# Groups 2 to 4 of an up projection as seven block products for eight, in an fp32 transformer block on one Trainium2 core

## The chip, the core and the metric

The kernel runs on one core of one Trainium2 chip. A core has TensorE (PE; its weight loads are listed apart as PEld), VectorE (DVE), ScalarE (ACT), GpSimd (POOL) and SyncE (SP), and 16 DMA engines. SP issues most loads; POOL issues the DMAs that add to what is already in device memory. The metric is the device time of one execution in microseconds (us).

## The reference

`hybrid_layer` is one transformer block on 512 tokens of width 1024, in fp32. All the input projections are one product, `proj = xn @ w_in`. A gated delta rule (8 heads) and a chunked retention (4 heads) follow, each with a gate and an output projection; then the mix, and an MLP:

```python
mix = (jax.nn.sigmoid(gate_a) * ya + jax.nn.sigmoid(gate_b) * yb) @ w_out
x = x + rmsnorm(mix, n_mix_post)

hn = rmsnorm(x, n_mlp_pre)
ff = jnp.square(jax.nn.relu(hn @ w_up)) @ w_down      # w_up 1024 x 4096, w_down 4096 x 1024
return x + rmsnorm(ff, n_mlp_post)
```

The change is in `hn @ w_up`.

## The kernel before

**Precision.** Each fp32 operand of a large product is split into a high part (rounded to the PE's fp32r) and a low part (the rest). `mm3` (L79) issues three matmuls: high x high, high x low, low x high. Activations are split once and stay on chip. Weights are split when they arrive: `weights` (L86) takes one of the `raw` buffers, has SP load 512 KB into it, and calls `split_weights` (L102), where ACT casts to `whi` (L109) and DVE subtracts to get `wlo` (L110). There are three slots each of `whi` and `wlo`, and two raw buffers, or four where a second pool is in `raw_pools`. The splits have a raised priority in the scheduler, which writes one fixed order of instructions for each engine; engines then work in that order and wait for each other by semaphores.

**Forms of product.** `feature_major` (L146) keeps weights stationary and streams the tokens: its results have features on the partitions. It runs over blocks of 2 x 128 rows of the weights, and inside over four groups of 128 features, each with its own PSUM bank of the pool `psm` (four banks, tag `mm`). `token_major` (L166) keeps activations stationary and streams the weights. A second PSUM pool, `psx`, has three banks with the tag `dl`.

**Seven products for eight.** The value and gate projections of the four retention heads, `values_and_gates` (L768), already use a scheme of the Strassen-Winograd kind. Tokens are halved (256 each), the 1024 rows of the weights are halved (512 each), and a pair of 512-wide column blocks makes up the two column halves: a 2 x 2 by 2 x 2 block product, done with seven block products instead of eight. It needs four sums of feature blocks (`feature_sums`, L752, kept on chip as high and low parts `s1` to `s4`) and four sums of weight blocks. The weight sums are made in device memory by `BlockSums` (L116): SP copies a block into a DRAM tile (`copy`, L127, in two parts), POOL issues DMAs that add other blocks or earlier sums to it (`adds`, L130, eight a set). The copies wait in a list, `trickle`; from the 14th load on each call of `weights` takes one off and puts it behind its own load on SP. The adds are handed out in order by `add_blocks` (L704), behind a marked DMA on POOL. `block_weights` (L139) loads and splits a summed block like any other.

**Order of the work around the change.** Delta rule (to about 500 us), then the retention heads one by one: `scores`, a gate product or the branch partial of the head before, `outputs` with `values_and_gates`. Then the second gate product, the last branch partial, and the mix. The output projection (`row_tiles`, L990) keeps its eight weight blocks split on chip (in buffers of tags `og`, `ff0`, `ff1` and `facc`), and for each tile of 128 tokens `mix_done` adds the residual, normalizes and transposes into `hn`.

The MLP (L1093 to L1136) goes in four groups of 1024 of the 4096 hidden features. For each group the up projection comes first, `feature_major` over two halves of 512 features with eight weight loads in all (the first half of the first group runs twice over 256 tokens, because its last tokens come late), and `square_relu` (L1083) takes each bank: ACT writes relu to `r`, DVE multiplies, ACT casts to the high part, DVE subtracts the low part. Then the down projection, `token_major` over two halves of 512 columns, is added to `facc`. Groups 1 and 3 keep their hidden features in `og` and `ff0`/`ff1`, groups 2 and 4 in the `actT` buffers. The last down projection is `row_tiles` again, with its weights kept in `og`, `ff0`/`ff1` and the place of `hn`; after each token tile comes the last norm and the store.

Of the kernel before, what the change touches and what calls it, by code (L numbers as in the profile page):

```python
# [60 lines left out]
def hybrid_block_kernel(ctx: ExitStack, tc: tile.TileContext, a: dict, out: bass.AP):  # L61
# [10 lines left out]
    trickle = []  # L72
    act = ctx.enter_context(tc.tile_pool(name="act", bufs=2))
# [12 lines left out]
    def weights(src, k0, nk, c0, ncols, keep=None):  # L86

        n = nk * ncols
        i = next(loads)
        pool, tag = raw_pools[i % len(raw_pools)]  # L90
        raw = pool.tile([P, 1024], F32, tag=tag, name="raw", bufs=2)
        load = nc.sync.dma_start(
            raw[:, :n].rearrange("p (k c) -> p k c", k=nk),
            src[k0 * P : (k0 + nk) * P, c0 : c0 + ncols].rearrange("(k p) c -> p k c", p=P),
        )
        if i >= 13 and trickle:
            sums, part, k = trickle.pop(0)
            with tc.issue_after(load.ins):
                sums.copy(part, k)
        return split_weights(raw, n, nk, keep, 200 if i >= 6 else 0)  # L100
# [38 lines left out]
    def block_weights(block):  # L139
# [4 lines left out]
        return split_weights(raw, 1024, 2)  # L144

# [299 lines left out]
    with tc.tile_pool(name="pa", bufs=1) as pa:  # L445
# [255 lines left out]
        vg_sums = [BlockSums(w_in, OFF_VB + h * 512, OFF_GB + h * 512, f"vg{h}") for h in range(4)]  # L701
        adds = itertools.chain.from_iterable(sums.adds() for sums in vg_sums)

        def add_blocks(mark, n):  # L704

            with tc.issue_after(mark.ins):
                for dst, src in itertools.islice(adds, n):
                    tc.keep_in_program_order(nc.gpsimd.dma_start(dst, src, accum_op=ALU.add))

# [26 lines left out]
    with tc.tile_pool(name="pb", bufs=1) as pb_:  # L736
# [10 lines left out]
        def quarter(kh, th):  # L747
            return [x[:, 4 * kh : 4 * kh + 4, 256 * th : 256 * th + 256] for x in xs]

        quarters = {"11": quarter(0, 0), "12": quarter(1, 0), "22": quarter(1, 1)}  # L750

        def feature_sums():  # L752
            full = [pb_.tile([P, 2, 4, 256], F32, tag=f"vr{i}", name="full") for i in range(2)]
            a11, a12, a21, a22 = full[0][:, 0], full[0][:, 1], full[1][:, 0], full[1][:, 1]
            for a, (kh, th) in ((a21, (0, 1)), (a22, (1, 1)), (a11, (0, 0)), (a12, (1, 0))):
                h, l = quarter(kh, th)
                nc.vector.tensor_tensor(a, h, l, ALU.add)
            nc.vector.tensor_tensor(a22, a21, a22, ALU.subtract)
            nc.vector.tensor_tensor(a21, a11, a21, ALU.subtract)
            nc.vector.tensor_tensor(a11, a22, a11, ALU.subtract)  # L760
            nc.vector.tensor_tensor(a12, a12, a11, ALU.add)
            for i, a in enumerate((a22, a11, a21, a12)):
                s = pb_.tile([P, 2, 4, 256], F32R, tag=f"xs{i}", name="xsum")
                nc.scalar.copy(s[:, 0], a)
                nc.vector.tensor_tensor(s[:, 1], a, s[:, 0], ALU.subtract)
                quarters[f"s{i + 1}"] = [s[:, 0], s[:, 1]]

        def values_and_gates(sums, c1, c2, g, out1, out2):  # L768
# [20 lines left out]
            def bank():  # L789
                return [psm.tile([P, T], F32, tag="mm", name="mm") for _ in range(2)]  # L790

            def plain(kh, c):
                return lambda ks: weights(w_in, 4 * kh + 2 * ks, 2, c, 512)

            def multiply(pss, x, wts, first):
                for ks in range(2):
                    product(pss, x, ks, wts(ks), first)

            def total(i):
                return lambda ks: sums.weights(i, ks)  # L800

            a = bank()
            multiply(a, "11", plain(0, c1), True)
            p1 = [tmp("p1") for _ in range(2)]
            with tc.high_priority(400):
                for t in range(2):
                    nc.scalar.copy(p1[t], a[t])
            multiply(a, "12", plain(1, c1), False)
            for t in range(2):
                out1(t, a[t])  # L810
            c = bank()
            multiply(c, "s1", total(1), True)
            with tc.high_priority(400):
                for t in range(2):
                    nc.scalar.copy(g[:, 2 + t, :], c[t])
            b = bank()
            multiply(b, "s3", total(3), True)
            p7 = [tmp("p7") for _ in range(2)]
            with tc.high_priority(400):
                for t in range(2):  # L820
                    nc.scalar.copy(p7[t], b[t])
            multiply(b, "s2", total(2), False)
            for t in range(2):
                nc.vector.tensor_tensor(p1[t], p1[t], b[t], ALU.add)
                nc.vector.tensor_tensor(p7[t], p1[t], p7[t], ALU.subtract)
                nc.vector.tensor_tensor(g[:, 2 + t, :], g[:, 2 + t, :], p1[t], ALU.subtract)
                out2(2 + t)
            d = [psx.tile([P, T], F32, tag="dl", name="dl", bufs=3) for _ in range(2)]
            multiply(d, "22", total(4), True)
            for t in range(2):  # L830
                nc.vector.tensor_tensor(p1[t], p1[t], d[t], ALU.add)
                out1(2 + t, p1[t])
            multiply(c, "s4", plain(1, c2), False)
            for t in range(2):
                nc.vector.tensor_tensor(g[:, t, :], c[t], p7[t], ALU.subtract)
                out2(t)
# [13 lines left out]
        def scores(h):  # L850
            dec = pb_.tile([P, T], F32, tag="dec", name="dec")
            decay = nc.gpsimd.dma_start(dec, a["c_decay"][h])
            if h in (1, 2):
                add_blocks(decay, 8 if h == 1 else 2)
# [69 lines left out]
        for h in range(4):  # L924
# [20 lines left out]
            if h == 0:  # L945
                raw_pools.append((pb_, "ych"))
            rows = outputs(h, scs)
# [4 lines left out]
        for half in range(2):  # L952
            ya.append(pb_.tile([P, 4, T], F32, tag=f"xs{2 + half}", name="ya"))
            nc.gpsimd.dma_start(ya[half], ya_d[:, half * 4 : half * 4 + 4, :])
# [24 lines left out]
    with tc.tile_pool(name="pm", bufs=1) as pm:  # L979
        def broadcast_row(vec, tag):  # L980
            w = pm.tile([P, D], F32, tag=tag, name=tag)
            nc.gpsimd.dma_start(w, vec.partition_broadcast(P))
# [62 lines left out]
        for t in range(4):  # L1045
            nc.gpsimd.dma_start(x2[:, t, :], x_d[t * P : (t + 1) * P, :])
# [36 lines left out]
        def square_relu(ps, hi, lo):  # L1083
            n = ps.shape[1]
            r = pm.tile([P, T], F32, tag="r", name="r", bufs=2)[:, :n]
            nc.scalar.activation(r, ps, AF.Relu)
            nc.vector.scalar_tensor_tensor(r, ps, 0.0, r, ALU.max, ALU.mult)  # L1087
            nc.scalar.copy(hi, r)
            nc.vector.tensor_tensor(lo, r, hi, ALU.subtract)

        wpost = broadcast_row(a["norm_mlp_post"][0], "post")
        facc = pm.tile([P, 4, D], F32, tag="facc", name="facc")
        for grp in range(4):  # L1093
            if grp % 2:
                whole = [act.tile([P, 8, T], F32R, tag="actT", name="actT") for _ in range(2)]
                ff = [[w[:, 4 * half : 4 * half + 4, :] for w in whole] for half in range(2)]
            else:
                ff = [
                    [act.tile([P, 4, T], F32R, tag="og", name="ff") for _ in range(2)],
# [64 lines left out]
```

## Time and profile before

| | |
|---|---|
| time, median of 3 runs | 1392.08 us (1391.12 to 1394.7) |
| profiled execution: time / span | 1392.33 us / 1390.6 us |
| granted PE clock, mean | 0.994 |
| PE / DVE / ACT / POOL busy | 1368.6 / 870.1 / 614.0 / 86.3 us |
| PE matmul instructions | 6670 |
| moved by DMA | 180.08 MB, mean 130 GB/s |
| up projection of group 2 (1121 to 1164.5 us): PE / DVE / ACT busy | 43.50 / 16.83 / 15.70 us |
| value-and-gate products of one head (679.26 to 717.34 us): PE / DVE / ACT busy | 38.08 / 24.42 / 21.53 us |

The span runs from the first to the last instruction; the time of an execution has a little around it. A row of a group of instructions gives its line in the code, its engine, the operation, what it writes and reads, how often, its busy time in us and the mean duration of one in ns. In a timeline row the first number is the start in us, the second the duration, and in brackets stands how long the engine was idle before and what released it. Matmuls are pipelined: their durations overlap, so their cost is the distance from start to start. A row of waits gives who waited for whom, the total in us, how many times, and the longest. A row of a stretch gives its bounds, its length, each engine's busy time with the count of instructions, the granted PE clock, the busy share of the DMA engines and GB/s.

### The profile page before, as it was taken

Reading aid. Unit: us, or ns where it says so; the run is one execution under the profiler, and the core shown is the slowest. Engines: PE = TensorE matmul, PEld = TensorE weight load, DVE = VectorE, ACT = ScalarE, POOL = GpSimd, SP = SyncE. Lnnn points to the kernel's source line nnn. Section 1 sums busy time; section 2 is a strip of 40 time slices with the busy share of each in tenths; the row PEclk is TensorE's granted clock in tenths of the full one; section 3 lists DMA queues with packets and bytes.
Section 4 is the critical chain, followed back from the end, with each engine's and each line's share of the span. In section 5 each row is a group of like instructions: output and inputs, shape, how many; then the busy total and the mean of one; then the engine's idle time right before and its main releaser. Section 6 shows DMA issues by size and latency. Waiting matters only on the chain.

```text
span 1390.6 us, 17607 instructions
## 1 busy us (share of the span) xinstructions
PE 1368.6 (98%) x6670; PEld 1123.1 (81%) x6670; DVE 870.1 (63%) x1539; ACT 614.0 (44%) x1134; POOL 86.3 (6%) x136
## 2 busy tenths in 40 slices
PE   8999999999999999999999999999999999999997
PEld 6888787778887888887888878878788888888886
DVE  5599889954665567477477486675685333343445
ACT  5777564624544323453553443543364333232331
POOL 1112300221021002000000000000000000000000
PEclk8999999999999999999999999999999999999999
DMA  5243624369367448762552443642724233233321
GB/s 159 72 141 120 190 92 158 117 147 235 107 129 159 121 144 168 193 206 76 157 154 84 151 121 91 200 133 68 236 91 135 93 94 104 92 103 94 106 76 61
DMA packets 88311, 180.08 MB, mean 130 GB/s; under 512 B 6079, under 2 KB 19537, under 8 KB 87714
## 3 DMA queue, kind: packets, MB, share of 16 engines
q1 hardware_dynamic: 77264, 148.39, 34.1%
q0 software_dynamic: 10240, 29.32, 10.8%
q8 instruction: 52, 0.85, 0.2%
q10 hardware_dynamic: 722, 1.25, 0.2%
q14 instruction: 33, 0.27, 0.1%
HBM read 173.17 MB, written 39.32 MB: 153 GB/s over the span
## 4 chain that ended last, share of the span: by engine, by line
PE 87%; DVE 6%; DMA 4%; ACT 2%; issue 1%; SPq 0%; DVEq 0%; ACTq 0%
PE mm L84 21%; PE mm L83 21%; PE mm L82 21%; PE mm L779 9%; PE tr L218 2%; DMA raw<-in_w_in_dram 2%; PE dl L779 2%; DVE wlo L110 1%; PE dl L84 1%; PE dl L82 1%; PE dl L83 1%; PE dl L670 1%; DVE c_y L406 1%; PE dl L642 1%; ACT whi L109 1%
## 5 line engine op out<-in xcount | busy, mean ns | idle before, releaser
L110 DVE TENSOR_TENSOR wlo<-raw,whi 128x1024 fp32r<-128x1024 f32 x232 | 283.5, 1223 | 334.9 <-ACT whi L109 334.0
L109 ACT CAST whi<-raw 128x1024 fp32r<-128x1024 f32 x232 | 244.0, 1053 | 452.4 <-PE mm L83 226.8
L84 PE MATMUL mm<-actT,wlo 128*128 128x512 f32 (+1 forms) x528 | 209.2, 396 | 0.0
L83 PE MATMUL mm<-actT,whi 128*128 128x512 f32 (+1 forms) x528 | 207.9, 394 | 1.1 <-DVE actT L252 1.1
L82 PE MATMUL mm<-actT,whi 128*128 128x512 f32 (+1 forms) x528 | 207.3, 394 | 0.6 <-ACT actT L251 0.6
L82 PEld LDWEIGHTS mm<-actT,whi 128*128 128x128 f32 x528 | 100.3, 190 | 20.6 <-ACT actT L251 1.1
L83 PEld LDWEIGHTS mm<-actT,whi 128*128 128x128 f32 x528 | 100.4, 190 | 20.4 <-DVE actT L252 1.3
L84 PEld LDWEIGHTS mm<-actT,wlo 128*128 128x128 f32 x528 | 100.7, 191 | 18.8
L82 PE MATMUL mm<-hn,whi 128*128 128x512 f32 (+1 forms) x288 | 105.6, 367 | 0.6 <-DVE r L1087 0.5
L83 PE MATMUL mm<-hn,whi 128*128 128x512 f32 (+1 forms) x288 | 105.3, 366 | 0.0
L84 PE MATMUL mm<-hn,wlo 128*128 128x512 f32 (+1 forms) x288 | 105.1, 366 | 0.0
L82 PE MATMUL mm<-og,whi 128*128 128x512 f32 x256 | 99.7, 390 | 0.6 <-DVE zz L369 0.6
L83 PE MATMUL mm<-og,whi 128*128 128x512 f32 x256 | 99.6, 389 | 0.0
L84 PE MATMUL mm<-og,wlo 128*128 128x512 f32 x256 | 99.6, 389 | 0.0
L82 PE MATMUL mm<-whi,actT 128*128 128x512 f32 x216 | 86.2, 399 | 0.0
L83 PE MATMUL mm<-wlo,actT 128*128 128x512 f32 x216 | 86.0, 398 | 0.0
L84 PE MATMUL mm<-whi,actT 128*128 128x512 f32 x216 | 85.6, 397 | 0.0
L779 PE MATMUL mm<-whi,xsum 128*128 128x512 f32 x256 | 80.1, 389 | 0.0
L406 DVE SCALAR_TENSOR_TENSOR c_y<-c_raw,convw,c_y 128x512 f32<-128x512 f32 x96 | 70.6, 752 | 3.4 <-ACT c_y L404 2.8
L82 PEld LDWEIGHTS mm<-hn,whi 128*128 128x128 f32 x288 | 54.3, 188 | 10.1 <-DVE r L1087 0.9
L83 PEld LDWEIGHTS mm<-hn,whi 128*128 128x128 f32 x288 | 54.3, 188 | 8.8
L84 PEld LDWEIGHTS mm<-hn,wlo 128*128 128x128 f32 x288 | 54.2, 189 | 8.8
(319 smaller groups left out, 2459.8 us busy)
## 6 DMA issues: line engine op xcount, KB each, us to landing
raw<-in_w_in_dram SPq DMA_DIRECT2D x105, 512.0 KB, 3.8
raw<-in_w_up_dram SPq DMA_DIRECT2D x36, 512.0 KB, 3.8
sums<-in_w_in_dram SPq DMA_DIRECT2D x32, 512.0 KB, 5.4
raw<-sums SPq DMA_DIRECT2D x32, 512.0 KB, 4.1
raw<-in_w_down_dram SPq DMA_DIRECT2D x32, 512.0 KB, 3.7
raw<-in_w_br_a_dram SPq DMA_DIRECT2D x16, 512.0 KB, 4.0
sums<-in_w_in_dram POOLq DMA_DIRECT2D x16, 512.0 KB, 12.3
sums<-sums POOLq DMA_DIRECT2D x16, 512.0 KB, 7.0
```

The costliest lines, as they stand in the source:

```text
L82: nc.tensor.matmul(ps, lh, rh, start=first, stop=False)
L83: nc.tensor.matmul(ps, lh, rl, start=False, stop=False)
L84: nc.tensor.matmul(ps, ll, rh, start=False, stop=last)
L109: nc.scalar.copy(hi[:, :n], raw[:, :n])
L110: nc.vector.tensor_tensor(lo[:, :n], raw[:, :n], hi[:, :n], ALU.subtract)
L218: nc.tensor.transpose(ps, src, ident)
L406: nc.vector.scalar_tensor_tensor(y, raw[:, j : j + T], tap(j), y, ALU.mult, ALU.add)
L642: nc.tensor.matmul(px[:, hh, :], rt[:, nn[hh], :], vx[:, hh, :], start=True, stop=True)
L670: nc.tensor.matmul(po[:, hh, :], at[:, 4 * hh + c, :], vn[:, hh, :], start=True, stop=True)
L779: m = nc.tensor.matmul(pss[t], lhs[i // 2], rhs[i % 2], start=first and k + i == 0, stop=k + i == 5, skip_group_check=not first,)
```

## The change

The scheme of the value and gate projections is made general and used for groups 2 to 4 of the up projection too.

- `seven` takes the place of the body of `values_and_gates` and serves both. The order of products is now 11, s2, 12, s1, s3, 22, s4 (it was 11, 12, s1, s3, s2, 22, s4). The products 11 and 12, and 22, go to `psx` banks, s2 with s3 and s1 with s4 to `psm` banks. Two pairs of temporaries are kept: `p1`, a copy of product 11 and later a running sum, and `u2` = p1 + product s2.
- For the up projection `up_product` keeps the weights stationary and streams 256 tokens: a PSUM bank holds two feature groups of 256 tokens side by side. `squares_up` takes the output blocks: the first (first token half, first column half) straight from PSUM as before; the other three with an addition or subtraction into `r` first.
- Three more `BlockSums` (`up_sums`, from `w_up`): 24 more copies on SP and 24 more adds on POOL, of 512 KB each. The copies are held back (`later_copies`) until the first retention head's gate products are done, and then follow the loads of scores and branch partials in heads 2 to 4 (loads inside `seven` take none). The adds come in batches: 4 behind the decay load of the fourth head, 10 behind the load of `ya`, 10 behind the residual loads and the row `wmlp`.
- Feature sums of `hn`: `sum_quarters` (8 DVE sums of 128 x 1024, 4 ACT casts, 4 DVE subtractions), put on DVE behind the first half of group 1. The plain sums stand in the place of `facc`, the split ones in `og` and `ff0`/`ff1` until the last group.
- All groups keep their hidden features in the `actT` buffers.

The diff, cut to its core:

```diff
-    def weights(src, k0, nk, c0, ncols, keep=None):
+    def weights(src, k0, nk, c0, ncols, keep=None, paced=True):
...
-        if i >= 13 and trickle:
+        if paced and i >= 13 and len(trickle) > later_copies[0]:
...
+    vg_sums = [BlockSums(w_in, OFF_VB + h * 512, OFF_GB + h * 512, f"vg{h}") for h in range(4)]
+    up_sums = [BlockSums(w_up, grp * 1024, grp * 1024 + 512, f"up{grp}") for grp in range(1, 4)]
+    adds = itertools.chain.from_iterable(sums.adds() for sums in vg_sums + up_sums)
...
+    def sum_quarters(xs, full, sums, quarters):
+        a11, a12, a21, a22 = full
+        for a, (kh, th) in ((a21, (0, 1)), (a22, (1, 1)), (a11, (0, 0)), (a12, (1, 0))):
+            h, l = quarter(xs, kh, th)
+            nc.vector.tensor_tensor(a, h, l, ALU.add)
+        nc.vector.tensor_tensor(a22, a21, a22, ALU.subtract)
+        nc.vector.tensor_tensor(a21, a11, a21, ALU.subtract)
+        nc.vector.tensor_tensor(a11, a22, a11, ALU.subtract)
+        nc.vector.tensor_tensor(a12, a12, a11, ALU.add)
+        for i, (a, s) in enumerate(zip((a22, a11, a21, a12), sums)):
+            nc.scalar.copy(s[:, 0], a)
+            nc.vector.tensor_tensor(s[:, 1], a, s[:, 0], ALU.subtract)
+            quarters[f"s{i + 1}"] = [s[:, 0], s[:, 1]]
+
+    def seven(src, c1, c2, sums, product, temp, out):
...
+        p1, u2 = [temp("p1") for _ in range(2)], [temp("u2") for _ in range(2)]
+        a = bank(psx)
+        plain(a, "11", 0, c1, True)
+        with tc.high_priority(400):
+            for t in range(2):
+                nc.scalar.copy(p1[t], a[t])
+        b = bank(psm)
+        summed(b, "s2", 2, True)
+        with tc.high_priority(400):
+            for t in range(2):
+                nc.vector.tensor_tensor(u2[t], p1[t], b[t], ALU.add)
+        plain(a, "12", 1, c1, False)
+        out(0, 0, a)
+        c = bank(psm)
+        summed(c, "s1", 1, True)
+        summed(b, "s3", 3, False)
+        with tc.high_priority(400):
+            for t in range(2):
+                nc.vector.tensor_tensor(p1[t], p1[t], b[t], ALU.add)
+        out(1, 1, c, p1, ALU.subtract)
+        d = bank(psx)
+        summed(d, "22", 4, True)
+        out(1, 0, d, p1, ALU.add)
+        plain(c, "s4", 1, c2, False)
+        out(0, 1, c, u2, ALU.subtract)
...
+        add_blocks(kept, 10)
...
+        with tc.issue_after(rows_in[1].ins):
+            add_blocks(residual, 10)
+        quarters = {"11": quarter(hn, 0, 0), "12": quarter(hn, 1, 0), "22": quarter(hn, 1, 1)}
...
+        def up_product(pss, x, ks, wts, first):
+            wh, wl = wts
+            xh, xl = quarters[x]
+            for f in range(4):
+                fs, ts = slice(f * P, (f + 1) * P), slice(256 * (f % 2), 256 * (f % 2) + 256)
+                for kk in range(2):
+                    k = 2 * ks + kk
+                    lhs, rhs = (wh[:, kk, fs], wl[:, kk, fs]), (xh[:, k, :], xl[:, k, :])
+                    for i in range(3):
+                        m = nc.tensor.matmul(
+                            pss[f // 2][:, ts], lhs[i // 2], rhs[i % 2],
+                            start=first and k + i + f % 2 == 0, stop=k + i == 5, skip_group_check=True,
+                        )
...
+        def squares_up(th, ch, pss, u=None, op=None):
+            for t in range(2):
+                dst = [w[:, 2 * t : 2 * t + 2, 256 * th : 256 * th + 256] for w in ff[ch]]
+                if u is None:
+                    square_relu(pss[t], *dst)
+                else:
+                    r = pm.tile([P, T], F32, tag="r", name="r", bufs=2)
+                    nc.vector.tensor_tensor(r, pss[t], u[t], op)
+                    square_relu(r, *dst, r)
...
         for grp in range(4):
+            whole = [act.tile([P, 8, T], F32R, tag="actT", name="actT") for _ in range(2)]
+            ff = [[w[:, 4 * half : 4 * half + 4, :] for w in whole] for half in range(2)]
+            if grp:
+                pinned = []
+                seven(
+                    w_up, grp * 1024, grp * 1024 + 512, up_sums[grp - 1], up_product,
+                    lambda name: pm.tile([P, T], F32, tag="u", name=name, bufs=4), squares_up,
+                )
```

145 lines of the change are left out of this document (59 added, 86 removed).

## The prediction

> **What bounds the kernel now.** I read the page's head, its shares of engines and the chain that ended last; then what TensorE (PE) waits for; then the stages around the change. The profiled execution took 1392.33 us, 1.73 us more than its span; the median of the three runs, 1392.08, is 0.25 us below it.
>
> ```profile
> span 1390.6 us, 17607 instructions
> PE 1368.6 (98%) x6670; PEld 1123.1 (81%) x6670; DVE 870.1 (63%) x1539; ACT 614.0 (44%) x1134; POOL 86.3 (6%) x136
> PE 87%; DVE 6%; DMA 4%; ACT 2%; issue 1%; SPq 0%; DVEq 0%; ACTq 0%
> PE tr L218 <- DVE o L916: 1.7, 4, 0.4
> PE mm L83 <- DVE keep L110: 0.8, 1, 0.8
> PE mm L82 <- DVE r L1087: 0.5, 1, 0.5
> PE mm L82 <- ACT keep L109: 0.4, 1, 0.4
> PE tr L218 <- DVE fw L1071: 0.3, 1, 0.3
> ```
>
> The last five rows are all of PE's waits from 560 us to the end: 3.7 us. Everything that the change touches lies there. So PE's own time sets the end, a matmul saved is time saved, and a new wait counts in full. Next is what one matmul costs: first and last row of two undisturbed stretches of PE's timeline, both in the first group of the up projection, where the weights are the stationary side as they will be in the new code.
>
> ```profile
> 1050.01 0.28 PE L83 MATMUL mm<-hn,whi 128*128 128x256 f32 x1
> 1052.89 0.28 PE L83 MATMUL mm<-hn,whi 128*128 128x256 f32 x1
> ...
> 1068.67 0.39 PE L83 MATMUL mm<-hn,whi 128*128 128x512 f32 x1
> 1077.51 0.39 PE L83 MATMUL mm<-hn,whi 128*128 128x512 f32 x1
> ```
>
> 24 starts of the 256-column kind in 2.88 us make 0.120 us each; 39 of the 512-column kind in 8.84 us make 0.2267 us. Half the columns cost 53%, not 50%: solved for a fixed part, 13.3 ns a matmul beside 0.4167 ns a column.
>
> **The change, part by part.** (1) *Matmuls.* A group of the up projection has 2 halves x 8 k x 4 features x 3 = 192 matmuls of 512 columns: 192 x 0.2267 = 43.5 us. Seven block products have 7 x 4 k x 4 features x 3 = 336 of 256 columns: 336 x 0.120 = 40.3 us. An eighth of the arithmetic is 5.4 us, but 144 further instructions take 144 x 13.3 ns = 1.9 us of it back. Gain 3.2 us a group, **9.6 us** in three. The new loop issues high x high, high x low, low x high as the old one does, so I take the row without an allowance.
>
> The Trainium skill, TensorE: Matmul & The Clock Gate, section Back-to-back issue gap, gives 262 cycles for 256 columns and 518 for 512, a fixed part of only 6 cycles. At 2.4 GHz (the page's warm clock) that would make the gain (192 x 518 - 336 x 262)/2400 = 4.8 us a group, 14.3 in all. The rows above give 288 and 544 cycles, so the trace disagrees, and the sum goes by the trace.
>
> (2) *Weight splits, DVE and ACT.* A group now has 8 blocks of 512 KB to split into high and low; it will have 14, one per 24 matmuls (2.88 us of PE).
>
> ```profile
> 1154.10 1.05 ACT L109 CAST whi<-raw 128x1024 fp32r<-128x1024 f32 x1 [4.38 <-PE mm L83]
> 1155.18 1.23 DVE L110 TENSOR_TENSOR wlo<-raw,whi 128x1024 fp32r<-128x1024 f32 x1 [4.21 <-ACT whi L109]
> 1340.37 4.63 DVE L110 TENSOR_TENSOR keep<-raw,keep 128x1024 fp32r<-128x1024 f32 x4 [0.23 <-ACT keep L109]
> 706.01 1.28 DVE L824 TENSOR_TENSOR p<-p,mm 128x512 f32<-128x512 f32 x2
> ...
> 715.79 1.23 DVE L110 TENSOR_TENSOR wlo<-raw,whi 128x1024 fp32r<-128x1024 f32 x1 [0.29 <-ACT whi L109]
> 1142.08 0.62 ACT L1088 CAST actT<-r 128x512 fp32r<-128x512 f32 x1 [0.25 <-DVE r L1087]
> ```
>
> Back to back a split costs DVE 4.63/4 = 1.16 us and an operation on 512 columns 1.28/2 = 0.64. A split starts when PE leaves its slot (first row) and is whole 2.3 us later. With three slots, it is needed two blocks after its start: 5.76 - 2.3 = 3.5 us to spare.
>
> DVE per group: 14 x 1.16, and on 512 columns 2 for u2, 2 for p1, 4 for the first output block and 6 for each of the three others, 26 x 0.64: 32.9 us of 40.3 (82%). ACT: 14 x 1.05 and 12 evictions of 0.62: 22.1 us. Neither becomes the bound on average; what counts is the crowd at the end. From the end of s3 (28.8 us into the group) DVE has p1 (1.3 us), the second output block (3.8) and two splits (2.3): 7.4 us in the 5.76 us of the sixth product. A bank is complete 1.4 us before its product ends, so DVE starts early: about 0.3 us of arrears. Then the third output block and two splits, 6.2 us in 5.76, leave some 0.7 us. At 40.3 us the down projection starts and wants the bank read by the last output after 12 matmuls (2.7 us). That bank is complete at 38.9 and is read about 1 to 2 us later: just in time. In the last group the down product uses two row tiles at once and wants it after 6 matmuls (1.4 us). I take 0.3 us a boundary, **+0.9 us**; bounds: 0, and 3.8 us a boundary (a whole output ahead of the read).
>
> (3) *Feature sums in group 1.* DVE gets 8 sums and 4 low parts of the form of the split, 12 x 1.16 = 13.9 us; ACT 4 x 1.05. They queue behind the last eviction of the first half:
>
> ```profile
> 1059.69 0.41 DVE L1089 TENSOR_TENSOR ff<-r,ff 128x256 fp32r<-128x256 f32 x1
> core 0: us, PE busy (x) PEld busy (x) DVE busy (x) ACT busy (x) POOL busy (x), PEclk, DMA share, GB/s
> 394.00:460.00 66.00, 64.35 (x291) 52.16 (x290) 35.79 (x73) 23.93 (x47) 11.67 (x12) 1.00 0.81 160
> 524.00:584.00 60.00, 60.00 (x267) 49.69 (x265) 36.55 (x40) 19.89 (x24) 9.22 (x10) 1.00 0.82 189
> 679.26:717.34 38.08, 38.08 (x169) 31.53 (x169) 24.42 (x27) 21.53 (x27) 0.00 (x0) 1.00 0.59 179
> 1029.40:1055.00 25.60, 24.68 (x201) 23.87 (x200) 20.72 (x45) 15.23 (x30) 0.53 (x1) 1.00 0.55 179
> 1055.00:1077.50 22.50, 22.50 (x104) 18.58 (x104) 10.30 (x17) 8.72 (x16) 0.00 (x0) 1.00 0.42 132
> 1121.00:1164.50 43.50, 43.50 (x193) 36.02 (x192) 16.83 (x20) 15.70 (x22) 0.00 (x0) 1.00 0.31 98
> ```
>
> 1060.1 + 13.9 + three splits (3.5) = 1077.5. The evictions of the second half come behind them; the first frees its bank at about 1078.2. The down projection wants that bank when the half ends, at 1078.0 (one matmul after the last PE row above is 1077.7, two 1078.0). **+0.6 us** with a hand-over; bounds 0 (evictions placed between the sums) and 3.8 (six operations late).
>
> (4) *Transfers.* SP gets 24 copies and 14 loads for 8 in each of three groups; POOL gets 24 adds. In a new group 14 x 0.52 MB in 40.3 us is 182 GB/s, the rate of the value-and-gate stage (679.26 to 717.34: 179 GB/s, share 0.59, PE never idle). That stage already reads summed blocks by the same route.
>
> ```profile
> sums<-in_w_in_dram SPq DMA_DIRECT2D x32, 512.0 KB, 5.4
> sums<-in_w_in_dram POOLq DMA_DIRECT2D x16, 512.0 KB, 12.3
> raw<-in_w_in_dram SPq DMA_DIRECT2D x4, 512.0 KB, 8.6
> raw<-sums SPq DMA_DIRECT2D x6, 512.0 KB, 4.2
> DMA to landing us min/median/max: 4.1/8.0/10.1
> SPq L92 <- DVE wlo L110: 887.0, 173, 25.8
> 524.56 3.57 POOL L708 DMA_DIRECT2D sums<-in_w_in_dram  x3
> 565.97 0.81 POOL L708 DMA_DIRECT2D sums<-sums  x1 [6.71 <-DMA sums<-sums]
> 908.07 0.53 POOL L954 DMA_DIRECT2D ya<-ya_d  x1 [15.71 <-PE mm L779]
> 970.98 0.53 POOL L1046 DMA_DIRECT2D acc<-in_x_dram  x1 [62.38 <-DVE tb L972]
> 992.67 0.53 POOL L982 DMA_DIRECT2D wmlp<-in_norm_mlp_pre_dram  x1
> ```
>
> The copies go one per load in scores and branch partials of heads 2 to 4, where a load lasts PE 24 x 0.2267 = 5.4 us; a copy lands in 5.4. Cover: four raw buffers. The third and fifth rows are of 394 to 460 us, where twelve adds ran: a load took 8.0 us and at most 10.1. With four raw buffers a load may take 4 x 2.72 - 2.3 = 8.6 us at the fastest pace before it eats into the 3 us kept by the split slots: covered to about 11.6. The risky places are four adds at the start of the third head's value-and-gate stage, and group 1's first half, where share 0.55 and the adds' 0.5 (0.81 less the 0.31 of a plain stage) fill the 16 engines: **+0.5 us**; bounds 0 and 3 (two loads 1.5 us beyond the cover of 8.6, with the splits' reserve used up).
>
> On POOL, eight adds took from 524.6 to 566, so ten take some 55 us: from 908 to about 963, before the residual loads queued behind them (970.98). The last ten follow wmlp, from 993 to about 1050, and what waits behind them is the last norm row, needed at the end. SP's in-order queue spends 887 us waiting for raw buffers, so the copies' issues find room; it is blocked by a late sum only when group 2 starts, at 1121: 70 us of margin.
>
> (5) *Value-and-gate products.* The same matmuls in another order; DVE 10 combining operations as before, ACT 4 copies fewer. PE has no wait inside the stage now. Nothing, between -1.7 (the four waits on o) and +3.2 (a wait like the longest of that list on a split, 0.8, once a head). The group results move to other buffers, all free a group earlier; and the last down product finds its kept slots freed by s2, s1, s3 and s4 in the order in which it needs them, the fourth three blocks (8 us) after s4. Nothing, cover: those 8 us.
>
> **Sum:** 1392.33 - 9.6 + 0.9 + 0.6 + 0.5 = 1384.7; less 0.25, **1384.5 us** as median.
>
> **The rivals.** *All of it hidden.* For it: in the value-and-gate stage DVE works without a pause from 706.01 us to 715.5 (the 0.29 us of idle before its row at 715.79 is the first) and PE does not wait. Against it: that crowd is smaller by four operations. 1392.1 - 9.6 = 1382.5, or 1380.8 if the waits on o go too.
>
> *The evictions eat the gain.* 2 to 3 us at each of the four boundaries of (2) and (3): 8 to 10 us, 1390 to 1392, no change. For it: 82% DVE, against 16.83 of 43.5 us now. Against it: banks complete early.
>
> *Slower: splits caught behind evictions.* DVE works in order. An output block goes DVE, DVE, ACT, DVE; with hand-overs of 0.25 a pair takes some 3 us. A split queued behind such a pair is late by that and has 3.5 us to spare, so one pair is survived, two are not. Three pairs stand in the last 12 us of a group; if two of them push a split by 2.5 us each, a group loses 5 us for its 3.2. It decides from 3.2 us of waits a group; with 5, and (3) and (4), 1392.1 + 5.4 + 1.1 = 1398.6. Against it: PE's empty list of waits in today's crowded stage.
>
> *The fixed part isn't paid.* If consecutive matmuls on the same high weights ran without it, the gain would be 5.1 to 5.4 us a group and the time near 1378. The page's cycle counts point that way (14.3 us: 1377.8). Against it: such pairs stand in both quoted stretches and pay.
>
> *It does not do what it says:* PE keeps the same time because blocks wait for sums. The margins of (4) speak against it; 1388 to 1392.
>
> **How the numbers follow.** My forecast 0.55, all hidden 0.14, evictions eat it 0.14 (0.02 of it still faster), no fixed part 0.03, not what it says 0.04, slower 0.10. Three runs of this kernel tell some 0.3%, 4.2 us, from no change. Faster 0.55 + 0.14 + 0.03 + 0.02 = 0.74, same 0.12 + 0.04 = 0.16, slower 0.10. The range reaches from all hidden, 1380.5, to the gain eaten, 1392: about 0.83. The forecast's own range is 1382.5 to 1387.
>
> **What will show it.** PE count 6670 + 432, busy time down by about 10 us; starts 0.12 us apart in the new products; an up group 40.3 us and a down group 43.5. Step (2) is right if PE waits under 1 us at each turn from up to down, (3) if it waits about 0.6 at the first turn, (4) if no PE wait is led back to a DMA after 757 us. The prediction is wrong if starts are 0.13 us or more apart (129.5 ns is break-even), or if PE waits for splits inside a product.

## The result

The changed kernel takes 1384.53 us (median of seven runs, 1381.41 to 1386.46) against 1391.29 us before (seven runs, 1387.5 to 1394.7): ratio 0.9947, 95% interval 0.9934 to 0.996. Five later runs gave 1384.46 us against 1391.63, ratio 0.994 [0.9923, 0.9957].

From the page of the changed kernel, its span, its busy times and the engines of the chain that ended last:

```profile
span 1382.8 us, 18650 instructions
PE 1361.0 (98%) x7102; PEld 1135.8 (82%) x7102; DVE 923.4 (67%) x1599; ACT 621.4 (45%) x1128; POOL 110.5 (8%) x160
PE 81%; DVE 9%; DMA 5%; ACT 3%; issue 1%; SPq 0%; DVEq 0%; ACTq 0%
```

432 matmuls more and 7.6 us less of PE; PE still sets the end. PE's waits from 560 us on, of the changed kernel (L84 is the second matmul of `mm3`, L111 the subtraction of a weight split, L1105 the multiplication in `square_relu`):

```profile
PE tr L289 <- DVE o L929: 1.6, 4, 0.4
PE mm L84 <- DVE keep L111: 1.6, 2, 1.1
PE mm L83 <- DVE r L1105: 0.8, 2, 0.5
PE tr L289 <- DVE fw L1088: 0.3, 1, 0.3
PE mm L83 <- ACT actT L1108: 0.2, 1, 0.2
```

4.5 us where it was 3.7. None is led back to a DMA, and none stands inside the seven products. Of the 1.6 us on `keep`, 0.48 us belong to the output projection ahead of the MLP (before: 0.8 and 0.4) and 1.07 us to the last down projection. To see where the 7.8 us between the two spans came from, I take the first matmul of each stage from PE's timeline. Before: start of the up projection of groups 1, 2 and 4, and of the down projection of group 1 (second row).

```profile
1029.38 0.28 PE L82 MATMUL mm<-hn,whi 128*128 128x256 f32 x1
1077.96 0.39 PE L82 MATMUL mm<-whi,ff 128*128 128x512 f32 x1
1121.48 0.39 PE L82 MATMUL mm<-hn,whi 128*128 128x512 f32 x1
1295.56 0.39 PE L82 MATMUL mm<-hn,whi 128*128 128x512 f32 x1
```

After, the same four, and as fourth of five the first matmul of group 2's down projection:

```profile
1028.42 0.28 PE L83 MATMUL mm<-hn,whi 128*128 128x256 f32 x1
1077.54 0.50 PE L83 MATMUL mm<-whi,actT 128*128 128x512 f32 x1 [0.37 <-DVE r L1105]
1121.21 0.40 PE L1127 MATMUL dl<-hn,whi 128*128 128x256 f32 x2
1161.52 0.40 PE L83 MATMUL mm<-whi,actT 128*128 128x512 f32 x1
1289.04 0.40 PE L1127 MATMUL dl<-hn,whi 128*128 128x256 f32 x2
```

| stage | before | after | difference |
|---|---|---|---|
| all that comes ahead of the MLP | 1029.38 | 1028.42 | -0.96 |
| group 1, up | 48.58 | 49.12 | +0.54 |
| group 1, down | 43.52 | 43.67 | +0.15 |
| groups 2 and 3, up and down | 174.08 | 167.83 | -6.25 |
| group 4 to the end of the span | 95.04 | 93.76 | -1.28 |
| from group 1 to the end | 361.22 | 354.38 | -6.84 |

In groups 2 and 3 an up projection lasts 40.31 us (1121.21 to 1161.52), 3.21 less than 43.52. The two down projections behind them lose 0.17 us together. The last group should have gained 3.21 too and kept 1.28. The first line is within chance: in the fourteen profiles of this study the MLP begins anywhere from 1026.0 to 1029.4 us, and an experiment whose code up to there is that of before began at 1026.72.

What happens in the last group? DVE's timeline of the changed kernel, chosen rows (L1142 combines a bank with `p1` or `u2` and so frees it; rows with `keep` are splits of the last down projection's eight weight blocks; the first row is the last sum into `p1`):

```profile
1318.62 0.68 DVE L209 TENSOR_TENSOR p<-p,mm 128x512 f32<-128x512 f32 x1
...
1322.09 1.22 DVE L111 TENSOR_TENSOR keep<-raw,keep 128x1024 fp32r<-128x1024 f32 x1
1323.23 1.22 DVE L111 TENSOR_TENSOR wlo<-raw,whi 128x1024 fp32r<-128x1024 f32 x1
...
1325.01 1.23 DVE L111 TENSOR_TENSOR keep<-raw,keep 128x1024 fp32r<-128x1024 f32 x1
1326.15 0.68 DVE L1142 TENSOR_TENSOR r<-mm,p 128x512 f32<-128x512 f32 x1
...
1328.79 0.69 DVE L1142 TENSOR_TENSOR r<-dl,p 128x512 f32<-128x512 f32 x1
...
1331.70 1.29 DVE L1109 TENSOR_TENSOR actT<-r,actT 128x512 fp32r<-128x512 f32 x2
1332.91 2.36 DVE L111 TENSOR_TENSOR keep<-raw,keep 128x1024 fp32r<-128x1024 f32 x2
1335.18 0.69 DVE L1142 TENSOR_TENSOR r<-dl,p 128x512 f32<-128x512 f32 x1
1335.78 0.68 DVE L1142 TENSOR_TENSOR r<-mm,u 128x512 f32<-128x512 f32 x1
```

and from PE's timeline the two waits, and from the stretches the crowd, changed kernel first, before's stretch last:

```profile
1335.32 0.50 PE L84 MATMUL mm<-keep,actT 128*128 128x512 f32 x1 [1.07 <-DVE keep L111]
1339.81 0.50 PE L83 MATMUL mm<-keep,actT 128*128 128x512 f32 x1 [0.21 <-ACT actT L1108]
1318.00:1331.00 13.00, 13.00 (x102) 12.62 (x102) 12.38 (x15) 8.16 (x10) 0.00 (x0) 1.00 0.74 243
1331.00:1345.00 14.00, 12.64 (x55) 9.38 (x55) 11.17 (x15) 5.36 (x8) 0.00 (x0) 1.00 0.12 39
...
1318.00:1339.20 21.20, 21.20 (x94) 17.37 (x93) 10.78 (x13) 9.26 (x13) 0.00 (x0) 1.00 0.41 137
```

DVE is busy 12.38 of 13.00 us, where it was busy 10.78 of 21.20. The splits of the kept blocks have a raised priority and stand ahead of the evictions. The second output's last combination has its inputs complete from 1319.30 on. Three kept splits come between (1319.22 to 1326.2), and it runs at 1326.15; s4, begun at 1323.59, wants that bank after 12 matmuls, at 1325.03. The third output's combinations run at 1328.79 and 1335.18, the second of them 3.8 us after s4's end (1331.42). Only behind it come the last output's, at 1335.78 and 1340.41, and these free two of the four `psm` banks that the down product uses; the third output stands in `psx`. The order written for PE has nine matmuls of the down projection in the gap in s4 (1325.03 to 1327.1). After s4 the down product has two banks, so PE soon comes to the fourth kept block, whose slot s4 frees, and waits 1.07 us for it.

### The profile page after: what moved, and what is told of

The parts are those of the page before. It is cut to its first block, busy times and chain, and to the rows that moved or that the text cites. A ratio compares the mean times of both kernels' runs of the same rounds, so it can differ in the third digit from the quotient of the medians.

```text
span 1382.8 us, 18650 instructions
## 1 busy us (share of the span) xinstructions
PE 1361.0 (98%) x7102; PEld 1135.8 (82%) x7102; DVE 923.4 (67%) x1599; ACT 621.4 (45%) x1128; POOL 110.5 (8%) x160
## 4 chain that ended last, share of the span: by engine, by line
PE 81%; DVE 9%; DMA 5%; ACT 3%; issue 1%; SPq 0%; DVEq 0%; ACTq 0%
PE mm L83 17%; PE mm L85 17%; PE mm L84 17%; PE mm L827 6%; PE dl L827 5%; PE mm L1127 4%; PE dl L1127 3%; DMA raw<-in_w_in_dram 3%; PE tr L289 2%; DVE wlo L111 2%; DVE c_y L477 1%; ACT whi L110 1%; PE dl L85 1%; PE dl L83 1%; PE dl L84 1%
## 5 line engine op out<-in xcount | busy, mean ns | idle before, releaser
L111 DVE TENSOR_TENSOR wlo<-raw,whi 128x1024 fp32r<-128x1024 f32 x250 | 305.5, 1223 | 293.9 <-ACT whi L110 291.9
L110 ACT CAST whi<-raw 128x1024 fp32r<-128x1024 f32 x250 | 262.8, 1052 | 465.8 <-PE mm L84 190.4
L84 PE MATMUL mm<-actT,whi 128*128 128x512 f32 (+1 forms) x528 | 207.9, 394 | 1.0 <-DVE actT L323 1.0
L83 PE MATMUL mm<-whi,actT 128*128 128x512 f32 x344 | 136.2, 396 | 0.4 <-DVE r L1105 0.4
L84 PE MATMUL mm<-wlo,actT 128*128 128x512 f32 x344 | 135.8, 395 | 0.0
L85 PE MATMUL mm<-whi,actT 128*128 128x512 f32 x344 | 135.0, 394 | 0.0
L84 PEld LDWEIGHTS mm<-actT,whi 128*128 128x128 f32 x528 | 100.4, 190 | 20.2 <-DVE actT L323 1.3
L84 PE MATMUL mm<-og,whi 128*128 128x512 f32 x256 | 99.7, 389 | 0.0
L83 PEld LDWEIGHTS mm<-whi,actT 128*128 128x128 f32 x344 | 64.6, 188 | 14.6 <-DVE r L1105 0.8
L85 PEld LDWEIGHTS mm<-whi,actT 128*128 128x128 f32 x344 | 64.6, 188 | 13.2
L84 PEld LDWEIGHTS mm<-wlo,actT 128*128 128x128 f32 x344 | 64.6, 188 | 12.8
L1127 PE MATMUL mm<-hsum,whi 128*128 128x256 f32 x384 | 69.6, 283 | 0.0
L827 PE MATMUL dl<-whi,actT 128*128 128x512 f32 x192 | 61.1, 389 | 0.0
L1127 PEld LDWEIGHTS mm<-hsum,whi 128*128 128x128 f32 x384 | 59.9, 192 | 0.1
```

The source lines that it names most:

```text
L83: nc.tensor.matmul(ps, lh, rh, start=first, stop=False)
L84: nc.tensor.matmul(ps, lh, rl, start=False, stop=False)
L85: nc.tensor.matmul(ps, ll, rh, start=False, stop=last)
L110: nc.scalar.copy(hi[:, :n], raw[:, :n])
L111: nc.vector.tensor_tensor(lo[:, :n], raw[:, :n], hi[:, :n], ALU.subtract)
L827: m = nc.tensor.matmul(pss[t], lhs[i // 2], rhs[i % 2], start=first and k + i == 0, stop=k + i == 5, skip_group_check=not first,)
```

## The experiments

Where a run has only one time, it is read by stages, which agree between runs to about 0.1 us (group 1 of the repeated changed kernel took 92.79 us both times) but for the last group: in the five profiles of kernels that leave it as in the changed kernel it takes 93.36 to 94.23 us.

**The price of a matmul.** In the kernel before, the up projection of groups 2 to 4 in halves of 256 columns:

```diff
-                    mm3(pss[f], ...)
+                    for i in range(2):
+                        ts = slice(256 * i, 256 * i + 256)
+                        for j in range(3):
+                            nc.tensor.matmul(pss[f][:, ts], (wh, wl)[j // 2][:, kk, fs], xs[j % 2][:, kt, ts], ...)
```

> The kernel before, with the same arithmetic and the same order of blocks, but each of the 192 matmuls of 512 columns in the up projection of groups 2 to 4 issued as two of 256 columns. Theory (a matmul costs 13.3 ns beside its columns, as before's two row stretches gave): an up group goes from 43.5 us to 384 x 0.120 = 46.1 us, three groups add 7.7 us, the time 1391.3 to 1399.0, a ratio of 1.0055. Rival (the fixed part is not paid where consecutive matmuls use the same high weights, or only a part of 6 cycles is): an up group stays at 43.5 to 44.0 us, the time within 1.4 us of before's, ratio 1.000 to 1.001.

Measured over four runs: 1399.52 us, ratio 1.0064 [1.0047, 1.0082]. The first matmul of group 2's up and of its down projection in this run:

```profile
1118.81 0.40 PE L161 MATMUL mm<-hn,whi 128*128 128x256 f32 x2
1164.88 0.40 PE L82 MATMUL mm<-whi,actT 128*128 128x512 f32 x1
```

46.07 us, 2.55 more than 43.52: 192 further matmuls at 13.3 ns. The fixed part is paid also where consecutive matmuls share their high weights, as the first two of each three do. The Trainium skill (TensorE: Matmul & The Clock Gate, Back-to-back issue gap) has 2.5 ns for it, by which three groups would add an estimated 1.4 us; this run, with 2.55 us in a group and so 7.65 in three, disagrees. (The medians differ by 8.1 us; the last group has a PE wait of 0.54 us besides.)

**The new value-and-gate order alone.** `up_sums` is empty, and the loop over the groups is that of before:

```diff
-    up_sums = [BlockSums(...) for grp in range(1, 4)]
+    up_sums = [BlockSums(...) for grp in range(0)]
```

> The changed order of the value-and-gate products alone: up projection, its weights and its features as before. Theory (step 5 of the prediction: nothing): groups 2 to 4 take 43.5 us each for the up projection as before, the four value-and-gate stages keep their length within 0.3 us, PE shows no wait in them, and the end comes within 1 us of before's. Rival 1 (the order itself brings something, since four ACT copies a head go): 0.4 us a head, 1.7 us in all, seen as a group 1 that starts up to 1.7 us earlier. Rival 2 (it costs): a PE wait of up to 0.8 us in every head.

1389.8 us in one run. From group 1 to the end 361.23 us, before 361.22. A retention head lasts 94.93 us (start of the products of values and scores 621.62, 716.55, 811.47, 906.44), before 95.1 and in the changed kernel 95.0: no new wait, and a gain of 0.2 us a head at most. Step 5's "nothing" holds for the value-and-gate part.

**No weight sums.** In place of the summed blocks, plain blocks of `w_up` are loaded, so these sums are missing from what is computed:

```diff
-    up_sums = [BlockSums(w_up, ...) for grp in range(1, 4)]
+    up_sums = [PlainBlocks(w_up, ...) for grp in range(1, 4)]     # no copies, no adds; loads of the same size
```

> The changed kernel without the 24 copies and 24 adds: in the place of the four sums of a group, plain weight blocks of w_up of the same size are loaded, so the weight sums are left out, while PE, DVE and ACT do the same instructions. Theory (the transfers of step 4 are hidden, so their 0.5 us was too much): every stage from 560 us on has its length within 0.3 us and the end is within 0.5 us of the changed kernel's. Rival (the transfers cost something that shows in no PE wait, for example slower loads behind which the splits run late): stages that hold adds, 585 to 780 us and 909 to 1085 us, are together 0.5 to 3 us shorter without them.

1384.6 us; from group 1 to the end 354.49 us (changed kernel 354.38), the last group 93.90 (93.76). Taking 48 transfers of 512 KB away changes no stage from group 1 on by more than 0.15 us. From the first value-and-gate stage's end (622.79) to group 1 (1028.41) it took 405.62, against 405.93 with the sums; 0.3 us, less than what chance does there. So the transfers are hidden, as far as one run can tell.

**Feature sums later.** All twelve operations behind the second half of group 1:

```diff
-                if half == 0:
+                if half == 1:
                     with tc.issue_after(done.ins):
```

> The changed kernel with the 12 feature-sum operations of group 1 behind the last eviction of its second half in place of its first. Theory (step 3: the 0.4 us wait at the first turn from up to down, and the slightly slower matmuls behind it, come from these operations): the wait of PE on r at 1077.5 us goes, and group 2 begins 0.4 to 0.7 us earlier; the down projection of group 1 has room for 13.9 us of DVE in 43.5 us. Rival (the crowd only moves): the 12 operations now stand ahead of the splits of the down projection's weights, one of which is needed each 2.7 us, and PE waits there by 2 to 5 us, so group 2 begins later than in the changed kernel.

1386.19 us. The wait at the first turn is gone, group 1's up projection takes 48.58 us as before. Its down projection takes 45.50. The row that shows why, and group 2's start:

```profile
1101.43 0.50 PE L83 MATMUL mm<-whi,actT 128*128 128x512 f32 x1 [1.66 <-ACT facc L1177]
1123.35 0.40 PE L1127 MATMUL dl<-hn,whi 128*128 128x256 f32 x2
```

The down projection's results go to `facc`, and the plain sums stand in that slot until the last low part is made, at 1099.87 us. The rival was right that the crowd only moves, but not by its mechanism: no split is late, a slot is.

**Feature sums in two parts.** Hence only the low parts behind the second half:

```diff
+        if part == 1:
+            low_parts(full, sums, quarters)
+            return
...
-                if half == 0: ... sum_quarters(hn, full, sums, quarters)
+                ... sum_quarters(hn, full, sums, quarters, half)    # sums in half 0, low parts in half 1
```

> The changed kernel with the feature sums of group 1 in two parts: the eight sums (9.3 us of DVE) behind the last eviction of the first half as now, the four low parts (4.6 us) behind the last eviction of the second half. Theory (step 3: the first turn waits because the evictions of the second half queue behind 13.9 us of sums and low parts): the wait on r at the turn goes and group 1, 92.79 us from the start of its up projection to that of group 2 (before: 92.10), takes 92.1 to 92.3 us; the low parts are done by 1083 us, before the first eviction of the down product into the slot of the full sums, so the wait of 1.7 us that all twelve caused in that place does not come. Rival (whatever stands behind the second half delays the down product's splits or that eviction): a wait of 0.5 to 1.7 us within the down product, 92.6 to 93.8 us.

1381.31 us in one run. Starts of group 1 and group 2:

```profile
1026.01 0.28 PE L83 MATMUL mm<-hn,whi 128*128 128x256 f32 x1
1118.09 0.40 PE L1135 MATMUL dl<-hn,whi 128*128 128x256 f32 x2
```

92.08 us, before's 92.10: all of step 3's cost is gone, though the low parts end at 1085.3 and not by 1083 us, and no PE wait is left between the two rows but the two of the norm and of the first token half that before has too.

**The last group.** Four edits, each alone or together. First the slot that s4 frees, used last:

```diff
+                wk.append(wk.pop(3))
```

> The changed kernel with the kept slot that the last product s4 of group 4 frees used by the last of the down product's eight weight blocks in place of its fourth. In the changed kernel the last group, from the start of its up projection to the end of the span, took 93.76 us, 1.9 more than before's 95.04 less the 3.2 of the matmuls; PE waited 1.07 and 0.21 us there for the split into that slot. Theory A (the slot comes free too late for the fourth block): both waits go and the last group takes 92.3 to 92.6 us. Theory B (DVE is full from 1318 to 1342 us and the splits stand ahead of the evictions, so any order of the slots ends at the same time): another PE wait of about the same size takes their place, and the last group stays at 93.5 to 94.0 us.

The last group takes 96.39 us (span 1383.9 less 1287.51), 2.6 more. The two waits are gone, and another is there:

```profile
1336.55 0.47 PE L83 MATMUL mm<-keep,actT 128*128 128x512 f32 x1 [3.08 <-DVE r L1142]
```

Now PE waits for a bank whose eviction is late. It is a bank of the last output. The late slot was the first thing that DVE's delay ran into, not the cause: theory B, and worse than its 93.5 to 94.0. Then the down projection behind s4:

```diff
-                row_tiles(w_down, ff_tile, grp * 8, lambda kt: wk[kt], ff_done)
+                with tc.issue_after(pinned[-1].ins):
+                    row_tiles(w_down, ff_tile, grp * 8, lambda kt: wk[kt], ff_done)
```

> The changed kernel with the last down product's matmuls behind the last matmul of s4, so that its nine early ones no longer run ahead of the end of s4. Theory A: s4 ends 2.07 us earlier (group start plus 40.3 us), its slot is free and its split done 2.07 us earlier, but the down product reaches its fourth block earlier relative to that too, since nine of its matmuls are no longer done: the wait of 1.07 us shrinks or stays, last group 92.5 to 93.8 us. Theory B: DVE's evictions of the third output come as late as before, PE wants their banks sooner, and waits for them 1 to 3 us after 6 matmuls: last group 93.8 to 95 us.

94.95 us (1381.8 less 1286.85). The wait comes earlier than either theory had it, inside s4:

```profile
1324.78 0.50 PE L1127 MATMUL mm<-hsum,whi 128*128 128x256 f32 x2 [1.78 <-DVE r L1142]
```

s4 is added to the bank from which the second output has first to be taken. The nine early matmuls of the changed kernel fill this wait; they are not its cause. (This expectation and the next speak of the third output's banks; the down product's `psm` banks are those of s3's product and of the last output.) With both edits:

> Both edits, the slot of s4 used last and the down product behind s4. Theory A: no wait on a kept split is left, last group 91.9 to 92.5 us, less than with the slot edit alone because nothing holds the banks of s4 back. Theory B: the down product wants the third output's banks 6 matmuls after s4 and DVE is 1 to 3 us late with them: 92.8 to 95 us, more than with the slot edit alone.

95.53 us: again 1.82 us inside s4, and 0.35 behind it. That refutes theory A, but theory B missed too: the time is above its 95 us, and less, not more, than with the slot edit alone (96.39). Last the priority of the splits:

```diff
-        return split_weights(raw, n, nk, keep, 200 if i >= 6 else 0)
+        return split_weights(raw, n, nk, keep, raised if i >= 6 else 0)     # raised = 0 for w_down's kept blocks
```

> The changed kernel with the eight kept splits of the down projections at ordinary priority in place of a raised one, so that DVE takes evictions that are ready first. Theory B (splits ahead of evictions cost the 1.9 us): the third output's evictions come 2 to 5 us earlier, the banks free with them, and the last group takes 92 to 92.8 us. Theory A (the slot of s4 is late, whatever the order): the split of the fourth block comes no sooner, its wait stays at about 1.1 us or grows by the 3 to 6 us of evictions that are now ahead of it, last group 93.7 to 97 us.

92.29 us (1381.2 less 1288.91); time 1382.94 us. The last combination of the second output and both of the third, from DVE's timeline of this run:

```profile
1321.62 0.69 DVE L1142 TENSOR_TENSOR r<-mm,p 128x512 f32<-128x512 f32 x1
...
1325.09 0.68 DVE L1142 TENSOR_TENSOR r<-dl,p 128x512 f32<-128x512 f32 x1
...
1328.03 0.68 DVE L1142 TENSOR_TENSOR r<-dl,p 128x512 f32<-128x512 f32 x1
```

They come 4.5, 3.7 and 7.2 us earlier than in the changed kernel, the first of them before s4 wants the bank, and the last output's 4.8 and 5.5 us earlier, at 1330.97 and 1334.90. No matmul of the down projection is drawn ahead, and one PE wait is left, 0.57 us for a bank. The fourth block's split is not the late one that theory A expects. DVE does the same work and is as full (22.92 of the 24 us from 1318 to 1342, with all eight kept splits; changed kernel 22.86). The order alone gives 1.47 us back, or 1.07 to 1.94 by the five profiles of the unchanged last group.

**GpSimd instead of DVE.** Every second low part of the eight kept blocks on GpSimd, with the raised priority:

```diff
-            nc.vector.tensor_tensor(lo[:, :n], raw[:, :n], hi[:, :n], ALU.subtract)
+            eng.tensor_tensor(lo[:, :n], raw[:, :n], hi[:, :n], ALU.subtract)     # nc.gpsimd for kt = 1, 3, 5, 7
```

> The changed kernel with the low parts of every second kept block of the down projections' last product and its like in group 4 (four of the eight, priority raised as in the changed kernel) subtracted on GpSimd in place of DVE, which takes 4.7 us out of DVE's full stretch from 1318 to 1342 us. Theory B (DVE's load in that stretch is what costs the 1.9 us): the last group goes from 93.76 to 92.0 to 92.9 us, also with the priority raised. Rival (GpSimd is so slow at it, 3 us or more a block, or slows DVE down beside it, that its blocks are the late ones): new waits on keep at the second, fourth or sixth block, last group 93.8 us or more.

1387.07 us, the last group 98.32 us (1385.3 less 1286.98). The rival was right in its second half: DVE is slowed down. GpSimd's rows, DVE's rows at the same time, and PE's wait:

```profile
1320.26 2.41 POOL L111 TENSOR_TENSOR keep<-raw,keep 128x1024 fp32r<-128x1024 f32 x1 [242.61 <-ACT keep L110]
1329.50 5.15 POOL L111 TENSOR_TENSOR keep<-raw,keep 128x1024 fp32r<-128x1024 f32 x2 [6.83 <-ACT keep L110]
...
1321.15 2.60 DVE L111 TENSOR_TENSOR wlo<-raw,whi 128x1024 fp32r<-128x1024 f32 x1 [0.44 <-ACT whi L110]
1332.37 3.36 DVE L111 TENSOR_TENSOR keep<-raw,keep 128x1024 fp32r<-128x1024 f32 x1
...
1334.70 0.50 PE L84 MATMUL mm<-keep,actT 128*128 128x512 f32 x1 [2.91 <-POOL keep L111]
```

A low part takes GpSimd 2.4 to 2.8 us, twice DVE's time but under the 3 us of the rival's first half, and DVE's own splits beside it take 2.60 and 3.36 us for 1.22. So this run does not say what less work on DVE would bring: what GpSimd takes off DVE, it takes from DVE in time.

**Both that helped.** Feature sums in two parts and the ordinary priority, beside the changed kernel once more:

> The two edits that helped, together: feature sums in two parts, kept splits of the down projections at ordinary priority. If the two losses are separate (group 1: 0.69 us, group 4: 1.5 of 1.9 us), group 1 takes 92.1 us, groups 2 and 3 stay at 83.9 us each, the last group takes 92.2 to 92.5 us: 352.2 us from the start of group 1's up projection to the end, 9.0 us less than before's 361.2 and 2.2 us less than the changed kernel's 354.4; the time near 1382.2, ratio to before 0.993 to 0.994. Rival (a lower priority of the splits also delays them behind the low parts in group 1's down product, or the run's other stages swallow it): no difference from the changed kernel, ratio 0.9947.

> The changed kernel once more, beside the combination on the same chip. Both theories: ratio to before 0.994 to 0.996, and from the start of group 1's up projection to the end of the span 354.2 to 354.6 us, of it 92.7 to 92.9 in group 1 and 93.6 to 93.9 in the last group; stages before that differ by up to 1 us from run to run, as they did in the earlier runs.

The combination takes 1381.19 us (six runs, 1379.28 to 1385.59), ratio to before 0.9928 [0.9908, 0.9948]; the changed kernel beside it 1384.46 (five runs), 0.994 [0.9923, 0.9957]. The intervals overlap; the stages, in one profile of the combination and two of the changed kernel, do not. Start of group 1 and of group 4 in the combination, span 1379.7:

```profile
1027.65 0.28 PE L83 MATMUL mm<-hn,whi 128*128 128x256 f32 x1
1287.54 0.40 PE L1135 MATMUL dl<-hn,whi 128*128 128x256 f32 x2
```

352.05 us from group 1 to the end, 92.16 of them in the last group; the changed kernel took 354.85 here (94.23 in the last group, more than was expected, with 0.28 us of wait inside s4) and 354.38 in its first profile. Of the 9.63 us that the matmuls save, the combination keeps 9.17.

## Why the prediction was right, and where it was not

The time came out as forecast, 1384.53 for 1384.5, but not all terms did; and the forecast stood on a median of 1392.08 that later runs put at 1391.3 to 1391.6. The change is worth 6.8 to 7.2 us, where the sum said 7.6. That the two times agree to 0.03 us is luck: a start some 0.5 to 0.8 us too high and a gain some 0.4 to 0.8 too large cancelled, and within the sum 0.5 us for transfers, which cost nothing, stood against a last turn put 1.6 us too low. What held is the mechanism of the large term and the path through PE.

- *(1) Matmuls, -9.6:* measured 3.21 us less in each of groups 2 and 3. PE's busy time fell by 7.6 and not by some 10 us. The first matmul behind a wait takes 0.34 us to the next one's start instead of 0.2267, the next five 0.228 to 0.237, and single ones in DVE's crowd 0.30 to 0.47; all of this counts as busy. It makes 1.1 us in groups 1 and 4 and 0.2 in groups 2 and 3, and 0.7 us more of busy time came ahead of the MLP. Halving the columns alone, without the scheme, gave the same fixed part. "The fixed part isn't paid" is refuted.
- *(2) Turns from up to down, +0.3 each:* mis-sized in both directions. The inner two cost 0.10 and 0.07 us, with no PE wait at all. The last cost 1.93 us, with PE waits of 1.07 and 0.21 us, so the prediction's own sign for this step (under 1 us at each turn) fails there. The step that failed is its count of DVE's work in the last group: "the third output block and two splits" leaves out that the eight kept splits of the last down projection fall into the same 24 us, 8 x 1.16 = 9.3 us, and stand ahead of the evictions. Before, only four of them came ahead of the end of the up projection (1314.09 to 1328.1), the other four behind it (1340.37 to 1345.0).
- *(3) Feature sums, +0.6:* 0.69 us, of it 0.37 as a wait at the turn, the rest in matmuls that follow each other a little more slowly around it and in the down projection. Moving the low parts took away all of it, so the queue on DVE was the cause, as argued. My reading of the cost as bounded by where evictions stand was right; the slot of `facc`, which binds the sums to a place before the down projection's first result, was not in it.
- *(4) Transfers, +0.5:* zero. The lower bound, 0, was the right end; the adds came later than I had them (the last ten behind the row of the last norm, from 1030.9 us), and nothing waited for them.
- *(5) Value-and-gate order and kept slots, nothing:* right for the first. For the second, "cover: those 8 us" failed: s4 ended 2.07 us later, since nine other matmuls ran inside it, DVE was behind, and PE waited 1.28 us. The slot was no cause, as its own experiment shows; it belongs to the DVE crowd above.

Of the rivals, "the evictions eat the gain" happened at one of four turns, where it took 1.9 of 3.2 us. "Splits caught behind evictions" had the right queue and the wrong order: evictions were caught behind splits. What stays open is how far less work on DVE in that crowd, rather than another order, would go, because the only other engine tried for it slowed DVE down; and why the last group of the same changed kernel took 93.76 and 94.23 us in two profiles.

## What to carry to other kernels

When PE gets faster, look at the last stage by itself. Here its work for the other engines was not that of the inner stages: the eight kept splits, spread over 31 us before (1314.1 to 1345.0), fell into 19 us (1319.2 to 1337.9). Where an in-order engine is full for some 20 us, as DVE was here, what counts is whose turn is first: give the raised priority to what frees a bank that PE wants next, not to splits that are needed some blocks later. If taking away the wait that the profile names makes the kernel slower, as with the slot of s4, that wait was a symptom; look for the engine that had no pause before it.

## What the runs showed of the hardware

Two engines that both read two operands from on-chip memory excluded each other. In the GpSimd experiment a DVE split that began at 1321.15 beside a GpSimd one (1320.26 to 1322.67) ended 1.08 us after that one, at 1323.75; another, begun at 1332.37, ended 1.08 us after GpSimd's pair (1329.50 to 1334.65), at 1335.73. DVE's multiplications `r<-r`, 0.68 us alone, show the same: those begun at 1329.55 and 1338.06 took 2.90 and 1.65 us and ended 0.55 us after the GpSimd operation that ran then. The combinations `r<-mm,u`, which read one operand from PSUM, kept their 0.68 us beside GpSimd (1336.86 and 1337.46). Equal remainders behind GpSimd's end fit a DVE that stood still until GpSimd was done, not one that ran slowly. The Trainium skill says this (SBUF — State Buffer, section SBUF: two separate sides): the port pair shared by the two is an exclusive lock, also for a DVE instruction with two SBUF inputs against a GpSimd one that reads SBUF, and the loser blocks fully. This run agrees, at up to 2.2 us an instruction (2.90 for 0.68).
